# Stick-breaking attention: splitting a pair of heads in one step, with the pieces placed by DMA

## The chip, the cores and the metric

The kernel runs on one core of a Trainium2 chip. The engines of the core are TensorE (PE in the profile; its weight loads are PEld), VectorE (DVE), ScalarE (ACT), GpSimd (POOL) and SyncE (SP), which issues the DMAs. The metric is the device time of one execution in microseconds; the time of a kernel is the median over its runs.

## What is computed

One layer of a hybrid decoder over 1024 tokens of 1024 channels in float32: parallel token mixing (attention, a state-space mixer and two gates), cross-attention into 256 memory tokens, and a dense feed-forward. The change lies in the attention of the first part, 16 heads of 64 channels:

```python
def stick_breaking_attention(q, k, v):
    # beta[t,s] = sigmoid(q_t.k_s / sqrt(d)); A[t,s] = beta[t,s] * prod_{s<j<t}(1 - beta[t,j]), s < t
    ...
    for blk in range(seq // SB_BLOCK):
        z = jnp.einsum('bhtd,bhsd->bhts', qf[:, :, t0:t1], kf[:, :, :t1])
        causal = jnp.arange(t1)[None, :] < (t0 + jnp.arange(SB_BLOCK))[:, None]
        log_1mb = jnp.where(causal, jax.nn.log_sigmoid(-z), 0.0)
        tail = lax.cumsum(log_1mb, axis=3, reverse=True)
        w = jnp.where(causal, jnp.exp(z + tail), 0.0)
        outs.append(jnp.einsum('bhts,bhsd->bhtd', w, vf[:, :, :t1]))
...
merged = jax.nn.sigmoid(ga) * (o_att @ w_br_att[l]) + jax.nn.sigmoid(gs) * (o_ssm @ w_br_ssm[l])
```

q, k and the gate inputs ga and gs are columns of one projection of the normed stream, `h @ w_in`.

## The kernel before

Float32 products are made of several products in the type fp32r. A tensor is split into a high part (a copy rounded to fp32r, mostly by ACT) and a low part (the tensor minus its high part, a subtraction mostly by DVE); `mm3` (L101) multiplies high by high, high by low and low by high.

The attention stage is L725 to L926. It works on eight pairs of heads, and on 1024 positions in two halves of 512.

*Projections.* `dense` (L747) makes 128 output channels, that is one pair of heads, for all positions: it loads and splits the weights, and then runs for each half 8 x 3 matmuls into one PSUM bank ("mm", two banks), after which an eviction function is called with the bank. `qk_proj` (L771) gives it two such functions. `ev_q` (L775) writes for each of the two heads one tile "qs" of 128 partitions: partitions 0 to 63 hold the high part of q (L783, ACT), partitions 64 to 127 its low part (L784, DVE). `ev_k` (L786) writes two tiles for each head: "kh" holds the high part of k in both halves of the partitions, "kl" the low part; ACT (L795) and DVE (L796) write partitions 0 to 63, and a DMA for each tile copies these to partitions 64 to 127 (L797, L798). So one matmul over 128 partitions with qs and kh, and one with qs and kl, give all four products of a score. Each of these eviction instructions handles 64 partitions of 512 elements; each half of q or k has two on ACT and two on DVE. The tiles of q and k have four buffers, two pairs.

*Gates.* `gate_proj` (L802) uses `dense` too; its eviction is a sigmoid on ACT into a tile "gt" (two buffers), which is stored (L806). The last four of the 16 blocks of gate channels (gates 12 to 15) are computed inside the attention stage, beside its last five steps.

*Scores and values.* `scores` (L826) computes for one block of 128 positions the products with the keys (L838, L839), takes the sigmoid on ACT (L840) and a running product by a scan on DVE (L841). `values` (L848) transposes the result with PE (L857), splits it into weights wth (ACT, L860) and wtl (DVE, L861) and multiplies with the differences of v (L869, L870) into the one PSUM bank "av". At the end of a half of a head the two halves of the bank's partitions are added: ACT copies the lower one into a tile with the tag "gt" (L877), DVE adds it into the pair's output tile "oT" (L878, two buffers; one tile for each half of the positions, shared by the two heads), and after the second head SP stores the tile (L880). `differences` (L811) loads v twice, shifted by one position (L817), subtracts on POOL (L818) and splits on POOL (L92, L99).

*Order.* The main loop runs over 32 steps m, a head and a half each; four steps make a pair. `interleave` (L892) mixes the values of step m, the scores of step m + 1 and a quarter of the projections of a later pair (`qk_quanta`, L900): the pair after the next one's first q half in the last step of a pair, then second q half, first k half and second k half in the next three. Pair 0 is projected ahead of the loop, and its projections and those of pair 1 begin before attention proper. From step 27 on the quarters are replaced by pieces of the gates 12 to 15. The instructions of each engine run in the order that a scheduler lays down ahead of the run, from a simulated timeline and the program order; `issue_behind` (L212) keeps the projections from running ahead of the attention matmuls. A tile that takes over a buffer waits until all readers of the tile before it are done, stores among them.

After the attention stage follows the state-space stage (from L935 on), whose first matmul against the decay rows is L1027; its tables are built by POOL (L971) and DVE (L965 to L974) in memory that the attention stage leaves.

Of the kernel before, what the change touches and what calls it, by code (L numbers as in the profile page):

```python
# [8 lines left out]
F32 = mybir.dt.float32  # L9
F32R = mybir.dt.float32r  # L10
# [6 lines left out]
P = 128  # L17
# [4 lines left out]
HALF = 512  # L22
# [13 lines left out]
def hybrid_block(ctx, tc, a, out, dbg=None):  # L36
# [214 lines left out]
    with ExitStack() as pa:  # L251
# [473 lines left out]
        with ExitStack() as p2:  # L725
# [45 lines left out]
            def qk_proj(hp):  # L771
                for j in range(2):
                    heads[2 * hp + j] = {}

                def ev_q(ps, half):  # L775
                    sl = slice(half * HALF, (half + 1) * HALF)
                    for j in range(2):
                        hd = heads[2 * hp + j]
                        if half == 0:
                            hd["q"] = mk(qk, [P, S], F32R, "qs")  # L780
                        pj = ps[j * HD:(j + 1) * HD]
                        q = hd["q"]
                        A.activation(q[0:HD, sl], pj, AF.Copy)  # L783
                        V.tensor_tensor(q[HD:P, sl], pj, q[0:HD, sl].bitcast(F32), ALU.subtract)  # L784

                def ev_k(ps, half):  # L786
                    sl = slice(half * HALF, (half + 1) * HALF)
                    for j in range(2):
                        hd = heads[2 * hp + j]
                        if half == 0:  # L790
                            hd["kh"] = mk(qk, [P, S], F32R, "kh")
                            hd["kl"] = mk(qk, [P, S], F32R, "kl")
                        pj = ps[j * HD:(j + 1) * HD]
                        kh, kl = hd["kh"], hd["kl"]
                        A.activation(kh[0:HD, sl], pj, AF.Copy)  # L795
                        V.tensor_tensor(kl[0:HD, sl], pj, kh[0:HD, sl].bitcast(F32), ALU.subtract)  # L796
                        nc.sync.dma_start(kh[HD:P, sl].bitcast(F32), kh[0:HD, sl].bitcast(F32))  # L797
                        nc.sync.dma_start(kl[HD:P, sl].bitcast(F32), kl[0:HD, sl].bitcast(F32))  # L798

                return dense(C_Q + hp * P, ev_q), dense(C_K + hp * P, ev_k)  # L800

            def gate_proj(gi):  # L802
                def ev(ps, half):
                    gt = mk(t2, [P, HALF], F32, "gt")
                    A.activation(gt, ps, AF.Sigmoid)
                    nc.sync.dma_start(g_d[gi * P:(gi + 1) * P, half * HALF:(half + 1) * HALF], gt)  # L806
                return dense(C_GA + gi * P, ev)
# [40 lines left out]
            def values(h, half, ns_):  # L848

                st = {}  # L850
                ni = 4 * (half + 1)

                def tr(i):
                    t0 = max(0, i - 4 * half)
                    pt = mk(pst, [P, HALF], F32, "tr")
                    for tb in range(t0, 4):
                        T.transpose(pt[:, tb * P:(tb + 1) * P], ns_[tb][:, i * P:(i + 1) * P], ident)  # L857
                    wh = mk(wt, [P, HALF], F32R, "wth")
                    wl = mk(wt, [P, HALF], F32R, "wtl")
                    A.activation(wh[:, t0 * P:], pt[:, t0 * P:], AF.Identity, bias=mone)  # L860
                    V.scalar_tensor_tensor(wl[:, t0 * P:], pt[:, t0 * P:], -1.0, wh[:, t0 * P:].bitcast(F32), ALU.add, ALU.subtract)  # L861
                    st[i] = (wh, wl, t0 * P)

                def av(i):
                    if i == 0:
                        st["po"] = mk(psv, [P, HALF], F32, "av")
                    po, vt = st["po"], heads[h]["v"]
                    wh, wl, off = st[i]
                    T.matmul(po[:, off:], vt[:, i, :], wh[:, off:], start=i == 0, stop=False)  # L869
                    marks.append(T.matmul(po[:, off:], vt[:, i, :], wl[:, off:], start=False, stop=i == ni - 1))  # L870
                    if i == ni - 1:
                        hp, j = h // 2, h % 2
                        if (hp, half) not in ots:
                            ots[hp, half] = mk(t2, [P, HALF], F32, "oT")
                        o = ots[hp, half]
                        tmp = mk(t2, [P, HALF], F32, "gt")[0:HD]
                        A.activation(tmp, po[HD:P], AF.Copy)  # L877
                        V.tensor_tensor(o[j * HD:(j + 1) * HD], po[0:HD], tmp, ALU.add)  # L878
                        if j == 1:
                            nc.sync.dma_start(o_d[hp * P:(hp + 1) * P, half * HALF:(half + 1) * HALF], o)  # L880

                def step(i):
                    def run():
                        if i < ni:
                            tr(i)
                        if i >= LAG:
                            av(i - LAG)
                    return run

                return [step(i) for i in range(ni + LAG)]  # L890
# [976 lines left out]
```

## Time and profile before

| what | value |
|---|---|
| median of 3 runs | 2595.1 us |
| lowest to highest | 2594.28 to 2597.31 us |
| the profiled execution's own time | 2590.97 us |
| its span in the profile | 2589.3 us |
| mean granted PE clock over the span | 0.992 |
| attention main loop | about 675 to 1103 us of the span |

In the profile a row of a timeline gives the start and the duration in us, the engine, the line of the kernel, the operation with the tiles that it writes and reads, and in brackets the idle time of the engine just before it with what ended that. A row of the chain of waits gives the engine and line that waited, what it waited for, the sum of the waits in us, their number and the longest. A row of the summed windows gives the stretch, its length, and then for PE, PEld, DVE, ACT and POOL the busy us with the number of instructions, then the granted PE clock, the mean busy share of the 16 DMA engines and the GB/s that they moved. A row of the groups gives line, engine, operation, tiles, shapes and count, then the busy sum in us, the mean in ns, and the idle time before with its causes.

### The profile page before, as it was taken

How to read it: one execution, taken by the hardware profiler on the slowest of the kernel's cores; microseconds unless marked ns; L12 is line 12 of the kernel's file. 1: busy time of each engine (PE TensorE's matmuls, PEld its weight loads, DVE VectorE, ACT ScalarE, POOL GpSimd, SP SyncE). 2: the span in 40 equal slices, each digit the busy share in tenths (PEclk: the TensorE clock that was granted, in tenths of full speed). 3: DMA queues.
4: the chain of work that ended last, by engine and by line, in shares of the span. 5: the costliest groups of instructions: out<-in, count | busy, mean ns of one | idle time of the engine just before them, and what ended most of it. 6: DMA issues, size and time to landing. Idle time of an engine off the chain costs nothing. (4 is left out here: it accounts for less than half of the span.)

```text
span 2589.3 us, 32651 instructions
## 1 busy us (share of the span) xinstructions
PE 2491.0 (96%) x12026; PEld 2061.8 (80%) x12026; DVE 1824.0 (70%) x2119; ACT 1149.1 (44%) x2052; POOL 881.1 (34%) x690
## 2 busy tenths in 40 slices
PE   8999999999999999979999999999999999999998
PEld 6778787887787788767888788887787888887776
DVE  7676777777588988678788654415459666666997
ACT  6333354655466665556544302314333333334433
POOL 5331544443121211145656231101114323323675
PEclk9999999999999999989999999999999999999999
DMA  6441443334422322255322452321232232234322
GB/s 228 148 141 49 134 145 99 108 98 122 114 74 61 86 66 74 83 167 194 110 90 75 146 175 94 118 62 49 83 117 74 78 98 74 81 98 164 130 98 98
DMA packets 244331, 278.54 MB, mean 108 GB/s; under 512 B 15039, under 2 KB 171848, under 8 KB 243786
## 3 DMA queue, kind: packets, MB, share of 16 engines
q1 hardware_dynamic: 244170, 276.45, 33.6%
q8 instruction: 95, 1.56, 0.2%
q14 instruction: 66, 0.54, 0.1%
HBM read 197.87 MB, written 70.13 MB: 104 GB/s over the span
## 5 line engine op out<-in xcount | busy, mean ns | idle before, releaser
L841 DVE TENSOR_TENSOR_SCAN n<-n,mask 128x128 f32<-128x128 f32 (+7 forms) x128 | 178.5, 1418 | 10.5 <-ACT n L840 9.7
L99 DVE TENSOR_TENSOR sw<-sf,sw 128x512 fp32r<-128x512 f32 x150 | 128.9, 872 | 65.1 <-ACT sw L96 64.5
L196 POOL TENSOR_TENSOR sf<-wr,wr 128x512 f32<-128x512 f32 x38 | 59.5, 1566 | 286.0 <-DMA wr<-in_w_gu_dram 138.4
L860 ACT ACTIVATE wth<-tr,mone 128x512 fp32r<-128x512 f32 x192 | 111.1, 581 | 74.8 <-PE tr L857 73.3
L96 ACT ACTIVATE sw<-sf 128x512 fp32r<-128x512 f32 x150 | 91.9, 626 | 98.6 <-PE mm L222 86.1
L861 DVE SCALAR_TENSOR_TENSOR wtl<-tr,wth 128x512 fp32r<-128x512 f32 x192 | 101.5, 546 | 40.1 <-ACT wth L860 38.7
L99 DVE TENSOR_TENSOR sw<-wr,sw 128x512 fp32r<-128x512 f32 x113 | 107.0, 950 | 31.6 <-ACT sw L96 31.5
L222 PE MATMUL mm<-h,sw 128*128 128x512 f32 x320 | 124.3, 389 | 1.8 <-DVE sw L99 1.8
L220 PE MATMUL mm<-h,sw 128*128 128x512 f32 x320 | 122.3, 390 | 3.1 <-ACT h L96 2.3
L96 ACT ACTIVATE sw<-wr 128x512 fp32r<-128x512 f32 x113 | 70.9, 629 | 122.5 <-PE mm L222 122.2
L221 PE MATMUL mm<-h,sw 128*128 128x512 f32 x320 | 124.5, 389 | 0.0
L102 PE MATMUL mm<-oth,bw 128*128 128x512 f32 (+1 forms) x320 | 122.3, 382 | 2.1 <-DVE a L1138 1.5
L104 PE MATMUL mm<-oth,bw 128*128 128x512 f32 (+1 forms) x320 | 119.2, 372 | 0.6 <-DVE bw L1125 0.4
L103 PE MATMUL mm<-otl,bw 128*128 128x512 f32 (+1 forms) x320 | 118.6, 371 | 0.0
L92 POOL TENSOR_SCALAR v<-va 128x512 fp32r<-128x512 f32 x16 | 21.0, 1317 | 274.9 <-PE av L870 147.9
L656 DVE SCALAR_TENSOR_TENSOR b<-b,prmT,b 128x1023 f32<-128x1023 f32 (+2 forms) x72 | 106.0, 1475 | 10.3 <-ACT b L654 9.8
L840 ACT ACTIVATE n<-sc 128x512 f32<-128x512 f32 (+1 forms) x192 | 89.2, 486 | 49.0 <-PE sc L839 25.2
L165 POOL TENSOR_SCALAR rstd<-ms 128x1 f32<-128x1 f32 x82 | 27.7, 338 | 239.3 <-ACT x L1359 101.5
L102 PE MATMUL p<-bw,h 128*128 128x512 f32 x256 | 98.9, 391 | 3.3 <-DVE x L1361 2.3
L104 PE MATMUL p<-bw,h 128*128 128x512 f32 x256 | 100.1, 392 | 0.0
L103 PE MATMUL p<-bw,h 128*128 128x512 f32 x256 | 99.8, 390 | 0.0
L198 POOL TENSOR_TENSOR sf<-wr 128x512 f32<-128x512 f32 x38 | 63.2, 1663 | 107.4 <-DVE sw L99 107.4
(592 smaller groups left out, 8180.1 us busy)
## 6 DMA issues: line engine op xcount, KB each, us to landing
wr<-in_w_gu_dram SPq DMA_DIRECT2D x80, 256.0 KB
wr<-in_w_in_dram SPq DMA_DIRECT2D x36, 512.0 KB
zr<-in_w_in_dram SPq DMA_DIRECT2D x32, 512.0 KB
gu_d<-t SPq DMA_DIRECT2D x44, 256.0 KB
wraw<-in_w_in_dram SPq DMA_DIRECT2D x20, 512.0 KB
xs_d<-b SPq DMA_DIRECT2D x32, 256.0 KB
s<-xs_d SPq DMA_DIRECT2D x32, 256.0 KB
s<-zs_d SPq DMA_DIRECT2D x32, 256.0 KB
```

The source lines that it names most:

```text
L96: A.activation(o, i, AF.Copy)
L99: eng.tensor_tensor(o, i, hi.bitcast(F32), ALU.subtract)
L102: first = T.matmul(ps, sh, mh, start=start, stop=False)
L103: T.matmul(ps, sh, ml, start=False, stop=False)
L104: T.matmul(ps, sl, mh, start=False, stop=stop)
L220: T.matmul(ps, w[0][:, k, :], b[0][:, k, :], start=first and k == 0, stop=False, skip_group_check=True)
L221: T.matmul(ps, w[0][:, k, :], b[1][:, k, :], start=False, stop=False, skip_group_check=True)
L222: T.matmul(ps, w[1][:, k, :], b[0][:, k, :], start=False, stop=last and k == 3, skip_group_check=True)
L656: V.scalar_tensor_tensor(acc[:, sh:], y[:, :S - sh], cw(3 - sh, f), acc[:, sh:], ALU.mult, ALU.add)
L841: V.tensor_tensor_scan(nt[:, 0:L][:, ::-1], nt[:, 0:L][:, ::-1], mask[:, S - L:][:, ::-1], 1.0, ALU.mult, ALU.max)
L860: A.activation(wh[:, t0 * P:], pt[:, t0 * P:], AF.Identity, bias=mone)
L861: V.scalar_tensor_tensor(wl[:, t0 * P:], pt[:, t0 * P:], -1.0, wh[:, t0 * P:].bitcast(F32), ALU.add, ALU.subtract)
```

## The change

For the pairs 1 to 7 (`hp > 0`) a new function `split` takes the whole bank of 128 partitions, both heads: one ACT copy into a tile "hT" (the high part) and one DVE subtraction into "lT" (the low part), one buffer each. DMAs then carry the pieces of 64 partitions to their places: for q two for each head (high part, low part), for k four for each head (each part into both halves of the partitions). Pair 0 keeps the old way. Tiles with the tags "oT" and "gt", with two buffers each, are replaced by "oT0" and "oT1", one buffer each, for the two halves; the late gates use these same tags, and the ACT copy of the finished output (L877) uses "hT". The sum of these tiles' memory is the same as before.

```diff
@@ qk_proj
+                def split(ps):
+                    hi, lo = [mk(t2, [P, HALF], F32R, n, bufs=1) for n in ("hT", "lT")]
+                    A.activation(hi, ps, AF.Copy)
+                    V.tensor_tensor(lo, ps, hi.bitcast(F32), ALU.subtract)
+                    return hi.bitcast(F32), lo.bitcast(F32)
+
                 def ev_q(ps, half):
                     sl = slice(half * HALF, (half + 1) * HALF)
+                    if hp > 0:
+                        parts = split(ps)
                     for j in range(2):
                         hd = heads[2 * hp + j]
                         if half == 0:
                             hd["q"] = mk(qk, [P, S], F32R, "qs")
-                        pj = ps[j * HD:(j + 1) * HD]
                         q = hd["q"]
-                        A.activation(q[0:HD, sl], pj, AF.Copy)
-                        V.tensor_tensor(q[HD:P, sl], pj, q[0:HD, sl].bitcast(F32), ALU.subtract)
+                        rows_ = slice(j * HD, (j + 1) * HD)
+                        if hp > 0:
+                            for r, t in enumerate(parts):
+                                nc.sync.dma_start(q[r * HD:(r + 1) * HD, sl].bitcast(F32), t[rows_])
+                        else:
+                            A.activation(q[0:HD, sl], ps[rows_], AF.Copy)
+                            V.tensor_tensor(q[HD:P, sl], ps[rows_], q[0:HD, sl].bitcast(F32), ALU.subtract)
 
                 def ev_k(ps, half):
                     sl = slice(half * HALF, (half + 1) * HALF)
+                    if hp > 0:
+                        parts = split(ps)
                     for j in range(2):
...
-                        pj = ps[j * HD:(j + 1) * HD]
                         kh, kl = hd["kh"], hd["kl"]
-                        A.activation(kh[0:HD, sl], pj, AF.Copy)
-                        V.tensor_tensor(kl[0:HD, sl], pj, kh[0:HD, sl].bitcast(F32), ALU.subtract)
-                        nc.sync.dma_start(kh[HD:P, sl].bitcast(F32), kh[0:HD, sl].bitcast(F32))
-                        nc.sync.dma_start(kl[HD:P, sl].bitcast(F32), kl[0:HD, sl].bitcast(F32))
+                        rows_ = slice(j * HD, (j + 1) * HD)
+                        if hp > 0:
+                            for d, t in zip((kh, kl), parts):
+                                for r in range(2):
+                                    nc.sync.dma_start(d[r * HD:(r + 1) * HD, sl].bitcast(F32), t[rows_])
+                        else:
+                            A.activation(kh[0:HD, sl], ps[rows_], AF.Copy)
+                            V.tensor_tensor(kl[0:HD, sl], ps[rows_], kh[0:HD, sl].bitcast(F32), ALU.subtract)
+                            for t in (kh, kl):
+                                nc.sync.dma_start(t[HD:P, sl].bitcast(F32), t[0:HD, sl].bitcast(F32))
@@ gate_proj
-                    gt = mk(t2, [P, HALF], F32, "gt")
+                    gt = mk(t2, [P, HALF], F32, f"oT{half}", bufs=1)
@@ values, av
                         if (hp, half) not in ots:
-                            ots[hp, half] = mk(t2, [P, HALF], F32, "oT")
+                            ots[hp, half] = mk(t2, [P, HALF], F32, f"oT{half}", bufs=1)
                         o = ots[hp, half]
-                        tmp = mk(t2, [P, HALF], F32, "gt")[0:HD]
+                        tmp = mk(t2, [P, HALF], F32, "hT", bufs=1)[0:HD]
```

## The prediction

> **What bounds the kernel now.** I read the page first, then the summed windows over the attention stage, then the chain of waits there, then the timelines of the places the waits point to.
>
> ```profile
> span 2589.3 us, 32651 instructions
> PE 2491.0 (96%) x12026; PEld 2061.8 (80%) x12026; DVE 1824.0 (70%) x2119; ACT 1149.1 (44%) x2052; POOL 881.1 (34%) x690
> ```
> ```profile
> 680.00:1030.00 350.00, 337.47 (x1837) 281.50 (x1836) 308.36 (x374) 216.46 (x421) 60.59 (x39) 1.00 0.26 71
> ```
>
> The change touches the projections of pairs 1 to 7, and these lie between about 680 and 1030 us. There PE is busy 337.47 of 350 us at full granted clock, and DVE 308.36 (88%). Over the whole span DVE is at 70%, so here it is much closer to its limit than on average. What can be won is PE's idle time in the window, 350 - 337.47 = 12.5 us, 0.48% of the span. No saving on DVE or ACT is worth more than that, however many instructions go. The waits of PE in this window:
>
> ```profile
> PE av L870 <- DVE wtl L861: 8.5, 12, 1.2
> PE mm L102 <- DVE qs L784: 2.7, 2, 1.4
> PE tr L857 <- DVE wtl L861: 1.1, 1, 1.1
> ```
>
> They make 12.3 of the 12.5 us, and all end on DVE. So DVE's queue sets the end here, at a few fixed places, while PE's own work sets the rest. The places, one period of a pair (some 50 us) taken as the example; first DVE and PE where the first k half is evicted:
>
> ```profile
> 908.24 0.68 DVE L796 TENSOR_TENSOR kl<-mm,kh 64x512 fp32r<-64x512 f32 x1
> ...
> 911.45 0.69 DVE L796 TENSOR_TENSOR kl<-mm,kh 64x512 fp32r<-64x512 f32 x1
> 912.07 3.66 DVE L841 TENSOR_TENSOR_SCAN n<-n,mask 128x768 f32<-128x768 f32 x2
> 915.76 0.62 DVE L861 SCALAR_TENSOR_TENSOR wtl<-tr,wth 128x256 fp32r<-128x256 f32 x2
> ```
> ```profile
> 890.24 0.39 PE L870 MATMUL av<-wtl,v 128*128 128x256 f32 x1 [0.23 <-DVE wtl L861]
> ...
> 903.25 0.50 PE L102 MATMUL mm<-t1h,whi 128*128 128x512 f32 x1 [1.36 <-DVE qs L784]
> 903.59 0.40 PE L103 MATMUL mm<-t1l,whi 128*128 128x512 f32 x1
> 903.82 0.39 PE L104 MATMUL mm<-t1h,wlo 128*128 128x512 f32 x1
> ...
> 916.24 0.39 PE L870 MATMUL av<-wtl,v 128*128 128x256 f32 x1 [1.23 <-DVE wtl L861]
> ```
>
> At 916.24 PE stood 1.23 us for a weight tile that DVE began at 915.76, behind two scans, behind the second head's k subtraction at 911.45. At 890.24 it is the same with 0.23 us, after the first q half. Twelve such waits sum to 8.5 us with 1.2 as the longest; six of each of the two sizes would be 8.8, so they alternate, one of each in a pair. At 903.25 PE stood 1.36 us for the second head's q subtraction itself, which sat behind a slow scan:
>
> ```profile
> 899.17 3.30 DVE L841 TENSOR_TENSOR_SCAN n<-n,mask 128x512 f32<-128x512 f32 x1
> 902.50 0.70 DVE L784 TENSOR_TENSOR qs<-mm,qs 64x512 fp32r<-64x512 f32 x1
> ...
> 950.55 1.21 DVE L841 TENSOR_TENSOR_SCAN n<-n,mask 128x512 f32<-128x512 f32 x1
> ```
> ```profile
> 898.99 2.40 POOL L818 TENSOR_TENSOR va<-va,vb 128x1024 f32<-128x1024 f32 x1 [4.57 <-DMA va<-v_d]
> ...
> 950.66 3.30 POOL L818 TENSOR_TENSOR va<-va,vb 128x1024 f32<-128x1024 f32 x1 [4.87 <-issue]
> ```
>
> The same scan takes 1.21 us one pair later. It is slow where POOL's subtraction of v began 0.18 us ahead of it, and quick where POOL began 0.11 us behind it; there POOL took 3.30 instead of 2.40.
>
> **The change, part by part.** Evictions. Of each q or k half two copies on ACT and two subtractions on DVE (64 rows each) become one of each with 128 rows.
>
> ```profile
> L784 DVE TENSOR_TENSOR qs<-mm,qs 64x512 fp32r<-64x512 f32 x28 | 19.3, 689 | 2.0 <-ACT qs L783 0.4
> L795 ACT ACTIVATE kh<-mm 64x512 fp32r<-64x512 f32 x28 | 16.6, 594 | 14.3 <-PE mm L104 13.2 <-DVE kl L796 0.7
> L861 DVE SCALAR_TENSOR_TENSOR wtl<-tr,wth 128x512 fp32r<-128x512 f32 x80 | 54.2, 679 | 25.6 <-ACT wth L860 25.1
> ```
> ```profile
> L805 ACT ACTIVATE gt<-mm x8: 588/598/602, 1030.1 to 1099.4; 128x512 f32<-128x512 f32 x8
> ```
>
> On DVE 128 rows of 512 from PSUM cost 0.679 us, 64 rows 0.689; on ACT 0.598 against 0.594. Rows are free, so half of the instructions go: 7 pairs x 4 halves = 28 on DVE x 0.689 = 19.3 us, and 28 on ACT x 0.594 = 16.6 us. On the path is only what stands in front of a PE wait. First k half: the 0.69 us at 911.45 goes from the front of the 1.23 us wait; I take 0.65 x 6 = 3.9 us (bounds 0, if something else fills the place, and 6 x 1.2 = 7.2). First q half: the 0.23 us vanishes, 6 x 0.22 = 1.3 us. Second q half: the two waits of together 2.7 us end on an instruction that is gone, but the transposed-tile work behind it is then next on DVE; I take 2.0 (bounds 0 and 2.7). The one wait of 1.1 us: half, 0.6. Second k half: no wait of PE ends there, so nothing. Sum: 3.9 + 1.3 + 2.0 + 0.6 = 7.8 us, with 0 and 12.5 as ends.
>
> Pieces by DMA. q gets 4 DMAs per half (none before), k 8 (4 before): 24 issues of SP for a pair in place of 8. What they cost is in the existing ones:
>
> ```profile
> 908.23 0.47 SPq L797 DMA_DIRECT2D kh<-kh  x1
> ```
> ```profile
> 908.00:910.00 2.00, 2.00 (x14) 1.70 (x13) 1.86 (x3) 2.00 (x6) 0.00 (x0) 1.00 0.28 65
> 910.00:912.00 2.00, 2.00 (x13) 1.68 (x12) 1.97 (x4) 1.95 (x5) 0.00 (x0) 1.00 0.29 67
> 912.00:914.00 2.00, 2.00 (x11) 1.67 (x10) 2.00 (x3) 1.69 (x4) 0.00 (x0) 1.00 0.59 135
> ```
>
> SP: 16 more x 0.47 = 7.5 us in 50; behind them on SP queue the loads of weights and v and the stores of output tiles, which come later by at most the 3.8 us of one half's eight issues. The DMA engines: 2.0 x (0.28 + 0.29 + 0.59) = 2.32 us for four pieces, 0.58 each; 16 more make 9.3 us in a period in which they are 26% busy. q and k of a pair are read only while the next pairs are worked on, so their landing is covered; without that cover the first scores of a pair would wait 3 to 5 us (next paragraph). Cost taken: 0.
>
> The shared buffer. The high part (hT) has one buffer, and the copy of the finished output (L877) now uses it too. So this copy waits until the pieces of the high part have landed; behind it on ACT stand the high parts of the transposed weights, and PE waits for those. The closest places are the second q half and the second k half:
>
> ```profile
> 895.10 0.57 ACT L783 ACTIVATE qs<-mm 64x512 fp32r<-64x512 f32 x1
> ...
> 901.49 0.59 ACT L877 ACTIVATE gt<-av 64x512 f32<-64x512 f32 x1 [0.69 <-PE av L870]
> ```
> ```profile
> 921.67 0.68 DVE L796 TENSOR_TENSOR kl<-mm,kh 64x512 fp32r<-64x512 f32 x1 [0.18 <-ACT kh L795]
> ```
> ```profile
> 927.77 0.59 ACT L877 ACTIVATE gt<-av 64x512 f32<-64x512 f32 x1 [1.28 <-PE av L870]
> ```
>
> The copy starts 901.49 - 895.67 = 5.8 us after the q high part is ready, and 927.77 - 921.67 = 6.1 us after that of k. Three q issues are 1.4 us, six k issues 2.8 us, and the last piece then needs about 2 us (the traffic of the issues up to 912.21 is over by 914). That is 3.4 and 4.8 us: covered, by 2.4 and 1.3 us. Cost 0; the cover can go (a rival below).
>
> Output tiles with one buffer each. Up to pair 6 nobody else wants oT0 or oT1. At the end the late gates do: gate 14 is evicted into them while pair 7 still holds them.
>
> ```profile
> 1077.10 0.60 ACT L805 ACTIVATE gt<-mm 128x512 f32<-128x512 f32 x1
> ```
> ```profile
> 1089.85 0.38 SPq L880 DMA_DIRECT2D o_d<-oT  x1
> ```
> ```profile
> 1092.76 0.53 POOL L971 MEMSET cb<- 128x512 f32 x1 [6.41 <-PE mm L103]
> ```
> ```profile
> 1099.53 0.75 DVE L974 CAST keyrows<-cb 128x512 fp32r<-128x512 f32 x2
> ```
> ```profile
> 1109.10 1.19 PE L1027 MATMUL dec<-colrows,keyrows 128*128 128x512 f32 x2 [4.28 <-DMA colrows<-sum_d]
> ```
>
> The eviction at 1077.10 must now wait for the store issued at 1089.85 to land, about 1092. Both PSUM banks of the projections are then held by gate 14, so the 48 matmuls of gate 15 (48 x 0.23 = 11 us, by the steps from 903.59 to 903.82) can't run under pair 7's last work. With them out of the way that store comes earlier, I take about 1089, and the last of the 48 ends near 1100 in place of about 1092.7 (when POOL's L971 was let go). L971 moves with it by 7.5 us. Its result is wanted at 1099.53, 6.8 us after its start; with L971 itself and a select between, some 5.5 us of that are slack, so 7.5 - 5.5 = 2 us reach the next stage, whose L1027 starts at 1109.10. Bounds: 0 (PE is idle there for 4.28 us anyway) and 11.
>
> Sum: -7.8 + 2.0 = -5.8 us. The profiled execution took 2590.97 us, its span 2589.3; the median of the three runs is 2595.1, 4.1 above. I carry that difference along: 2595.1 - 5.8 = 2589.3 us.
>
> **The rivals.** *The gates give it back.* The end of the stage costs 6 to 11 us: the chain behind L971 then moves as a whole. For it: all 48 matmuls are displaced for certain. Against: the 5.5 us of slack. Price: -7.8 + 8 = 0, 2595.
>
> *The slow scan in every pair.* POOL's start is within 0.2 us of the scan's in both pairs shown, so any shift can turn it. In six pairs in place of two, four more scans are 3.30 - 1.21 = 2.09 us longer, of which PE showed 1.36 where it was hit: +5.4, and the 2.0 of the second q half is lost: -5.8 + 7.4 = +1.6, 2597. The Trainium skill ("SBUF — State Buffer", section "SBUF: two separate sides") calls the pair of ports that DVE and GpSimd share an exclusive lock: whichever instruction starts first holds it to its end. By that rule the loser is late in every pair and only who loses can change; the trace agrees with both orders (a scan of 3.30 us, a subtraction of 3.30 us).
>
> *Slower: hT holds the output copy.* The second q half's pieces are issued just when v, an output tile and weights are in flight:
>
> ```profile
> 898.00:900.00 2.00, 2.00 (x14) 1.57 (x13) 2.00 (x4) 0.54 (x1) 1.01 (x1) 1.00 0.98 282
> ```
>
> If they queue behind that traffic, which ends at about 900.2, four pieces end at 902.5, 1 us after the copy's turn at 901.49; it decides from a landing later than 5.8 us after the high part. With 1 us at both close places of 7 pairs: 14 us, -5.8 + 14 = +8, 2603.
>
> *The freed time does not reach PE*: something else on DVE fills each place and only the tail's cost is left. 0 to +2, 2596; the two scans at 912.07 speak for some of it.
>
> **How the numbers follow.** About 0.2% (5.2 us) is what a measurement of this kernel can tell from no change. Forecast 0.48: own range -12 to -3; 0.41 of it faster, 0.07 within. Gates 0.17 (0.13 within, 0.04 slower). Slow scan 0.12 (0.10 within, 0.02 slower). hT 0.15 (0.04 within, 0.11 slower). No relief 0.08 (within). Faster 0.41, same 0.42, slower 0.17. The range goes from -13 (all of PE's idle time) to +7.
>
> **What would show it.** Right: 28 fewer evictions on DVE and on ACT between 680 and 1030; PE's idle time there down from 12.5 to about 5 us, its wait for qs gone, that for wtl after the first k half near 0.6; the output copy (L877 before) not waiting for a DMA; the first matmul of the next stage (L1027, now 1109.10) about 6 us earlier, in spite of gates that end later. Wrong: waits of ACT for DMAs that read hT or lT, with PE waiting for ACT behind them; a gap of PE between the last output and the next stage that grows by more than 5 us; scans of 3.3 us in each pair.

## The result and the profile after

The changed kernel takes 2599.26 us (median of 22 runs) where the kernel before takes 2592.93 (22 runs on the same chip): ratio 1.0027, interval [1.0021, 1.0033], so it is slower by some 6.3 us. The forecast was 5.8 us faster. The time lies inside the stated range, on the other side of zero.

The page of the changed kernel, its summed window over the same stretch as before, and PE's chain of waits there. Lines have moved by 19: L860 is the scan (L841 before), L876 the transposes, L879 and L880 the transposed weights, L888 and L889 the value products, L896 the output copy, L897 the output's add, L824 the late gates, L777 and L778 the new split.

```profile
span 2597.2 us, 32736 instructions
```
```profile
680.00:1030.00 350.00, 334.00 (x1803) 278.82 (x1803) 291.19 (x339) 194.50 (x389) 60.17 (x39) 1.00 0.44 109
```
```profile
PE av L889 <- DVE wtl L880: 7.0, 10, 0.9
PE av L888 <- DVE oT L897: 4.2, 7, 0.6
PE tr L876 <- DVE wtl L880: 3.9, 6, 0.8
```

DVE's busy time fell from 308.36 to 291.19 us and ACT's from 216.46 to 194.50: the evictions did go. Yet PE's idle time rose, from 12.5 to 350 - 334.00 = 16.0 us. The waits for qs are gone, as forecast, and the longest for wtl fell from 1.2 to 0.9, where the forecast had 0.6. In their place PE waits for the output's add (L897) and, six times, ahead of the transposes. What is new on ACT and DVE, from their chains of waits in the same stretch:

```profile
ACT hT L777 <- DVE oT L897: 7.3, 12, 1.0
...
ACT hT L777 <- DMA kh<-hT: 3.3, 5, 1.8
...
DVE lT L778 <- DMA kl<-lT: 5.6, 4, 2.7
```

None of these is the wait that the prediction priced: the output copy (L896) waits for no DMA here. It is the split that waits, first for the reader of the output copy (the add), then for the pieces of the split before it. One place in full, from the timeline; it is the second k half of the pair that had its first k half at 861:

```profile
868.30 0.60 ACT L896 ACTIVATE hT<-av 64x512 f32<-64x512 f32 x1 [0.30 <-PE av L889]
...
870.97 0.39 PE L104 MATMUL mm<-b22h,wlo 128*128 128x512 f32 x1
...
876.75 0.60 ACT L896 ACTIVATE hT<-av 64x512 f32<-64x512 f32 x1 [0.18 <-PE av L889]
...
877.52 0.69 DVE L897 TENSOR_TENSOR oT<-av,hT 64x512 f32<-64x512 f32 x1
...
878.24 0.60 ACT L777 ACTIVATE hT<-mm 128x512 fp32r<-128x512 f32 x1 [0.18 <-DVE oT L897]
...
882.59 1.23 SPq L812 DMA_DIRECT2D kl<-lT  x2
...
884.32 0.60 ACT L777 ACTIVATE hT<-mm 128x512 fp32r<-128x512 f32 x1 [0.33 <-DMA kh<-hT]
...
885.70 0.69 DVE L778 TENSOR_TENSOR lT<-mm,hT 128x512 fp32r<-128x512 f32 x1 [0.98 <-DMA kl<-lT]
```

The projection's last matmul (L104) starts at 870.97, and its bank could be split then. But the split stands behind a second output copy (876.75), and that copy's add (877.52) must read hT first: the split comes at 878.24, some 7 us late. The program explains the place: `interleave` puts the output copy of this step at 6.5/7 = 0.93 of the step and this split at 7.5/8 = 0.94, while the other three splits of a pair stand ahead of the copy of their step. In the changed kernel, where the two share hT, the split keeps that place in all six pairs of the window. Its eight pieces are issued until 883.8, so they still hold hT and lT when the next pair's first q half is due, and that split waits for two DMAs (884.32, 885.70). One late split makes the next one late.

Of the twelve waits of the split for the add, six are of 0.18 us, at this place: the loss there is in the order and not in the wait. The other six, of about 1.03, are at the second q half, where the split stands behind the output copy of the step before it:

```profile
744.96 0.69 DVE L897 TENSOR_TENSOR oT<-av,hT 64x512 f32<-64x512 f32 x1
...
745.74 0.60 ACT L777 ACTIVATE hT<-mm 128x512 fp32r<-128x512 f32 x1 [1.03 <-DVE oT L897]
```

Two more things of the prediction's list are in this trace. The slow scan:

```profile
749.32 2.40 POOL L837 TENSOR_TENSOR va<-va,vb 128x1024 f32<-128x1024 f32 x1 [4.67 <-DMA va<-v_d]
749.85 2.95 DVE L860 TENSOR_TENSOR_SCAN n<-n,mask 128x512 f32<-128x512 f32 x1
```

A scan of that size behind POOL's subtraction is slow in five of six pairs, in place of two. They take 2.84 to 3.07 us, in place of 1.2. And the late gates:

```profile
1104.36 0.84 POOL L990 MEMSET cb<- 128x512 f32 x1 [18.17 <-PE mm L103]
...
1110.47 0.60 ACT L824 ACTIVATE oT<-mm 128x512 f32<-128x512 f32 x1 [4.10 <-DMA o_d<-oT]
1116.34 0.60 ACT L824 ACTIVATE oT<-mm 128x512 f32<-128x512 f32 x1 [5.27 <-DMA g_d<-oT]
```

They wait for stores as forecast, and the memset that POOL does once the last of the projections' matmuls are through (L971 before, at 1092.76) comes at 1104.36.

### The profile page after: what moved, and what is told of

The parts are those of the page before. It is cut to its first block, busy times and chain, and to the rows that moved or that the text cites. A ratio compares the mean times of both kernels' runs of the same rounds, so it can differ in the third digit from the quotient of the medians.

```text
span 2597.2 us, 32736 instructions
## 1 busy us (share of the span) xinstructions
PE 2492.4 (96%) x12026; PEld 2065.4 (80%) x12026; DVE 1815.5 (70%) x2091; ACT 1129.1 (43%) x2024; POOL 888.5 (34%) x690
## 5 line engine op out<-in xcount | busy, mean ns | idle before, releaser
L860 DVE TENSOR_TENSOR_SCAN n<-n,mask 128x128 f32<-128x128 f32 (+7 forms) x128 | 188.7, 1497 | 13.2 <-ACT n L859 13.1
L879 ACT ACTIVATE wth<-tr,mone 128x512 fp32r<-128x512 f32 x192 | 111.5, 584 | 78.0 <-PE tr L876 76.1
L880 DVE SCALAR_TENSOR_TENSOR wtl<-tr,wth 128x512 fp32r<-128x512 f32 x192 | 101.8, 544 | 53.2 <-ACT wth L879 52.5
L104 PE MATMUL mm<-oth,bw 128*128 128x512 f32 (+1 forms) x320 | 119.7, 374 | 2.0 <-DVE bw L99 1.2
L92 POOL TENSOR_SCALAR v<-va 128x512 fp32r<-128x512 f32 x16 | 12.2, 762 | 278.7 <-PE av L889 164.5
L876 PE MATMUL tr<-ident,n 128*128 128x128 f32 x576 | 95.6, 274 | 5.2 <-DVE wtl L880 5.2
L104 PE MATMUL p<-bw,h 128*128 128x512 f32 x256 | 100.1, 392 | 0.0
```

Of the source, the lines that this page charges most:

```text
L104: T.matmul(ps, sl, mh, start=False, stop=stop)
L860: V.tensor_tensor_scan(nt[:, 0:L][:, ::-1], nt[:, 0:L][:, ::-1], mask[:, S - L:][:, ::-1], 1.0, ALU.mult, ALU.max)
```

## The experiments

Every experiment was timed in five rounds beside the kernel before on the same chip, whose median there lay between 2592.26 and 2594.03. The table holds the ratios, and from one profile each the time from the first value product to the last (L888, "attention"), from there to the first product with the key rows (L1046), from there to the end, PE's idle time between 680 and 1030, and the number of slow scans (over 2.8 us in place of 1.2) there.

| kernel | us | ratio to before, interval | attention | to key rows | rest | PE idle | slow scans |
|---|---|---|---|---|---|---|---|
| before | 2592.93 | | 406.1 | 11.2 | 1480.2 | 12.5 | 2 |
| e8 (same instruction order) | 2592.61 | 1.0001 [0.9991, 1.0011] | 409.9 | 13.4 | 1481.7 | 16.3 | 4 |
| after | 2599.26 | 1.0027 [1.0021, 1.0033] | 411.1 | 12.6 | 1480.2 | 16.0 | 5 |
| e13 (after again) | 2599.40 | 1.0025 [1.0015, 1.0035] | 413.0 | 12.3 | 1478.3 | 17.7 | 5 |
| e1 | 2602.38 | 1.0034 [1.0022, 1.0046] | 411.1 | 11.8 | 1482.7 | 16.4 | 5 |
| e2 | 2599.03 | 1.0025 [1.0013, 1.0036] | 407.5 | 13.8 | 1477.3 | 13.6 | 2 |
| e3 (no subtraction) | 2600.08 | 1.0028 [1.0016, 1.0040] | 404.5 | 11.7 | 1478.7 | 14.4 | none |
| e4 (no subtraction) | 2604.68 | 1.0048 [1.0033, 1.0063] | 409.6 | 11.9 | 1477.8 | 16.9 | none |
| e5 | 2583.37 | 0.9966 [0.9954, 0.9979] | 401.6 | 13.0 | 1477.9 | 8.2 | 0 |
| e6 | 2582.82 | 0.9961 [0.9948, 0.9973] | 399.1 | 13.5 | 1472.6 | 7.9 | 0 |
| e14 (e6 again) | 2583.75 | 0.9962 [0.9948, 0.9976] | 399.4 | 13.3 | 1475.3 | 9.4 | 1 |
| e7 | 2598.70 | 1.0024 [1.0015, 1.0033] | 413.2 | 10.7 | 1482.5 | 16.8 | 5 |
| e9 | 2597.41 | 1.0013 [1.0001, 1.0025] | 406.6 | 13.2 | 1481.3 | 14.9 | 3 |
| e10 | 2595.00 | 1.0000 [0.9989, 1.0012] | 404.8 | 13.1 | 1479.4 | 10.4 | 2 |
| e11 | 2593.74 | 0.9995 [0.9986, 1.0004] | 406.2 | 13.2 | 1479.8 | 11.6 | 1 |
| e12 | 2614.72 | 1.0089 [1.0066, 1.0112] | 434.4 | 14.2 | 1477.9 | 28.8 | 0 |
| e15 | 2596.24 | 1.0011 [1.0000, 1.0021] | 408.7 | 13.6 | 1477.4 | 15.5 | 5 |

How much one profile can say is in the first two rows. The instructions of e8 stand in the same order on every engine as those of the kernel before, and their medians agree, but the profiled execution of e8 (2600.47 us, 7.9 above its median) is 9.4 us longer in span and 3.8 us in attention. So a difference of a few us between two single profiles is nothing; below, times are compared by medians, and profiles by the number and kind of their waits. Up to about 1025 us the orders fall into groups: before, e2, e8 and e9 are alike, and so are after, e13 and e15, and e5, e6 and e14.

**The tail, and the slow scan.** These are the two rivals that the trace seemed to speak for. e1 takes the late gates off the output tiles:

```diff
-                    gt = mk(t2, [P, HALF], F32, f"oT{half}", bufs=1)
+                    gt = mk(t2, [P, HALF], F32, ("lT", "hT")[half], bufs=1)
```

> The changed kernel, but the late gates are evicted into lT and hT, which are idle by then, and not into oT0 and oT1. Theory 'tail' (gate 14 waits for pair 7's output stores, so gate 15 and the tables of the next stage come late): the last gate matmul is done near 1093 to 1097 us of the span instead of 1104.4, L1046 starts 3 to 5 us earlier than 1117, the time falls by 3 to 4 us from 2599 to about 2595.5. Rival 'shared hT' (all the loss is made between 680 and 1030): nothing after 1030 us gets shorter by more than 1 us, time 2598 to 2600. Both expect the waits before 1030 us unchanged.

Measured 2602.38, not faster than the changed kernel and over both expectations. This did not free the gates, it moved them to two other tiles with one buffer; e15 below does it better.

e2 makes only the second part of the change on the kernel before: the two output tiles with one buffer, used by the late gates too.

```diff
-                    gt = mk(t2, [P, HALF], F32, "gt")
+                    gt = mk(t2, [P, HALF], F32, f"oT{half}", bufs=1)
...
-                            ots[hp, half] = mk(t2, [P, HALF], F32, "oT")
+                            ots[hp, half] = mk(t2, [P, HALF], F32, f"oT{half}", bufs=1)
```

> The kernel before with one part of the change alone: output tiles oT0 and oT1 with one buffer each, used by the late gates too; the evictions of q and k and the copy into its own tile stay as before. Theory 'tail': slower than before by 3 to 4 us (2596 to 2597), with gate 14's sigmoid waiting for stores of oT and POOL's L971 waiting for PE until after 1100 us; the stretch 680 to 1030 us as before. Rival 'shared hT': no more than 1 us slower than before.

Measured 2599.03, 5.9 us over its reference of 2593.14 [3.4 to 9.3]. Read by itself this says that the output tiles cost as much as the whole change and that the split gains nothing. Later runs showed that this reading was wrong.

e3 and e4 leave POOL's subtraction of v out of the kernel before and of the changed kernel, so that no scan can be slowed by it; the values are then not differences.

```diff
-                    G.tensor_tensor(va, va, vb, ALU.subtract)
```

> The kernel before without POOL's subtraction of the shifted v (L818): v is used unsubtracted, so that piece of the computation is left out. Theory 'slow scan' (a scan of 512 that meets this subtraction takes 2.9 to 3.3 us instead of 1.2 and PE waits): all scans of 512 near 1.2 us, PE's two waits for qs gone, 2 to 4 us faster than before. Rival: the scan's delay is hidden by other work, within 1 us of before.

> The changed kernel without POOL's subtraction of the shifted v (L837), that piece of the computation left out in the same way. Theory 'slow scan': the five slow scans between 680 and 1030 us return to 1.2 us, and the time falls by 5 to 8 us from 2599, so that the distance to the kernel before without the subtraction is 2 to 4 us in place of 6.3. Rival 'shared hT' and 'tail' alone: the time falls by no more than the same edit takes from the kernel before, distance 5 to 7 us.

Both came out slower than with the subtraction, 2600.08 and 2604.68, against what was expected; the first value product starts 9.6 and 7.0 us later in them (701.4 and 700.3 us). In both profiles the granted clock is 0.83 between 680 and 700 us, where it is 1.00 with the subtraction, and PE waits there some 5 us for the DMAs of kl; what brings this about is not settled. What they do tell: no scan is slow in e4, and its PE still idles 16.9 us, with the same waits of the split on ACT (lines after the one left out are one lower):

```profile
ACT hT L777 <- DVE oT L896: 7.2, 12, 1.0
```

And the distance between them is 4.6 us, close to the 6.3 with the subtraction; in attention it is 5.1 us without it and 5.0 with it. So the slow scans do not make most of the difference. What was left was that row.

**Who shares what.** e5 changes one name: the output copy gets a slot of the ring of four low weight tiles.

```diff
-                        tmp = mk(t2, [P, HALF], F32, "hT", bufs=1)[0:HD]
+                        tmp = mk(wt, [P, HALF], F32, "wtl")[0:HD]
```

> The changed kernel, but the output copy takes a slot of the low weight tiles' ring (four buffers) in place of hT; nothing else. Theory 'shared hT' (split and output copy hold each other's buffer, and that took the relief back): the split of the second k half no longer comes after the output copy, the waits of ACT's split for the output's add (7.3 us between 680 and 1030) are gone, the stretch from the first to the last value product falls from 411.1 to about 406, and the time from 2599 to about 2595. Rival 'pieces': it is the pieces of the split itself that hold hT and lT until they land (5.6 + 3.3 us of waits): these stay, the stretch stays near 411, the time near 2599. Rival 'redrawn order': the schedule comes out different with every edit and its luck is worth some 5 us; then the time may be anywhere from 2593 to 2603 whatever those waits do.

Measured 2583.37: 8.9 us under the kernel before and some 15 under the changed kernel, nearly four times the 4 us expected of it. The window, ACT's waits and PE's wait for the add, and the place shown above, one pair's second k half:

```profile
680.00:1030.00 350.00, 341.80 (x1866) 287.91 (x1865) 285.28 (x347) 199.56 (x401) 59.72 (x39) 1.00 0.45 114
```
```profile
ACT hT L777 <- PE mm L104: 17.8, 21, 3.0
```
```profile
PE av L888 <- DVE oT L897: 3.2, 6, 0.5
```
```profile
862.26 0.60 ACT L896 ACTIVATE wtl<-av 64x512 f32<-64x512 f32 x1 [0.31 <-PE av L889]
...
864.93 0.39 PE L104 MATMUL mm<-b22h,wlo 128*128 128x512 f32 x1
...
865.36 0.60 ACT L777 ACTIVATE hT<-mm 128x512 fp32r<-128x512 f32 x1 [1.62 <-PE mm L104]
...
871.51 0.60 ACT L896 ACTIVATE wtl<-av 64x512 f32<-64x512 f32 x1 [0.19 <-PE av L889]
```

The split now comes 0.43 us after the start of the last matmul, before the second output copy and not behind it. It waits for nothing but PE: the waits for the add are gone, and so are those for the pieces, although hT and lT still have one buffer each. PE idles 8.2 us in place of 16.0; 3.2 of these are waits for the output's add, which the kernel before did not have. Rival *pieces* falls with this: they held hT and lT only because the split before was late.

e6 also takes the late gates off, into the ring of the high weight tiles:

```diff
-                        tmp = mk(t2, [P, HALF], F32, "hT", bufs=1)[0:HD]
+                        tmp = mk(wt, [P, HALF], F32, "wtl")[0:HD]
...
-                    gt = mk(t2, [P, HALF], F32, f"oT{half}", bufs=1)
+                    gt = mk(wt, [P, HALF], F32, "wth")
```

> The changed kernel, with the output copy in a slot of the low weight tiles' ring and the late gates in slots of the high weight tiles' ring, so that hT holds nothing but the split and the one-buffer output tiles nothing but outputs. Theory 'shared buffers' (hT and the late gates together): the time falls by the 4 us of hT and by the 2 us at the end of the stage, to about 2593, level with the kernel before or below it; the late gates end some 7 us earlier. Rival 'pieces': 2597 (only the 2 us of the end). Rival 'redrawn order': anywhere from 2593 to 2603.

Measured 2582.82, the fastest median of all, but only 0.6 us under e5. Their intervals overlap almost wholly.

e7 is the split alone, with its parts in the two rings of weight tiles and gates, outputs and copy as in the kernel before:

```diff
-                    hi, lo = [mk(t2, [P, HALF], F32R, n, bufs=1) for n in ("hT", "lT")]
+                    hi, lo = [mk(wt, [P, HALF], F32R, n) for n in ("wth", "wtl")]
...
```

> The split alone: the kernel before with both heads split at once and moved by DMA, the high and low parts in slots of the two rings of weight tiles (four buffers each); output tiles, gates and output copy stay in their two-buffer tiles as before. Theory 'shared buffers': with nothing shared the forecast relief arrives, 5 to 8 us under the kernel before, 2586 to 2589. Rival 'pieces': the split gains nothing on its own, 2593 to 2598, since the pieces hold ring slots for 5 us and the weight tiles of the transposes wait for them. Rival 'redrawn order': from 2590 to 2600.

Measured 2598.70. The rival *pieces* named the mechanism, and both chains of waits show it: now it is the weight tiles that wait until the pieces have left their slots. On ACT and on DVE:

```profile
ACT wth L879 <- DMA qs<-wth: 9.9, 3, 4.7
```
```profile
DVE wtl L880 <- DMA qs<-wtl: 16.8, 5, 4.9
```

The output copy bears a ring slot (its reader follows within a few us), the split's parts do not (a queue of pieces reads them). What reads a slot matters, and not only how many there are.

e8 is the other half of e2: output tiles with one buffer each, gates left alone.

```diff
-                            ots[hp, half] = mk(t2, [P, HALF], F32, "oT")
+                            ots[hp, half] = mk(t2, [P, HALF], F32, f"oT{half}", bufs=1)
```

> The kernel before with the output tiles as two tiles of one buffer each and nothing else; gates keep their own two-buffer tile. Theory 'late gates' (the cost of 5.9 us of the output-tile part alone came from the gates evicted into these tiles): no cost is left, 2592 to 2594. Rival 'one buffer': the tiles themselves cost, because the add of the next pair waits for the store of the last: 2597 to 2599 as with the gates. Rival 'redrawn order': anything from 2590 to 2600.

Measured 2592.61 against 2592.26: nothing. The order of the instructions is that of the kernel before. So what e2 cost came with the gates. The profile of e8 also shows how far one order can vary: twice as many slow scans as before, and PE's wait for the second q half with them.

```profile
PE mm L102 <- DVE qs L784: 5.7, 4, 1.5
```

**Is it the split, and which of its halves.** e5 differs from the kernel before in the split, in where the copy lies, and in the output tiles of e2, which gained nothing there. e9 is the control for the copy: the kernel before with only the output copy in the ring.

```diff
-                        tmp = mk(t2, [P, HALF], F32, "gt")[0:HD]
+                        tmp = mk(wt, [P, HALF], F32, "wtl")[0:HD]
```

> The control: the kernel before, with nothing changed but that the output copy takes a slot of the low weight tiles' ring instead of a 'gt' tile. Theory 'the split pays once hT is its own': this does nothing, 2590 to 2595, first to last value product near 406, and the gain of 9 us of the version with the copy in its own slot is the split's. Rival 'the copy's slot pays': the gain comes from where the copy lies and not from the split; then this kernel is near 2584 too, with a stretch near 401.

Measured 2597.41, slower by 0.13% (0.3 to 6.5 us) and not faster, which was not expected either. So the gain of e5 does not come from where the copy lies; it is the split's. The instructions of e9 stand in the order of the kernel before up to 1039 us and in another after that, beside the late gates: an edit that touches no gate redraws the end of the stage, and a few us can come from that alone.

e10 and e11 are e5 with only the k halves, or only the q halves, split for both heads at once; the condition of the other function is made false in both its places. The first place in e10:

```diff
 def ev_q(ps, half):
...
-                    if hp > 0:
+                    if hp > 7:
```

> The changed kernel with the output copy in its own slot, and only the k halves split for both heads at once; the q halves are evicted head by head as before. Theory 'terms of the forecast' (k 3.9 of the relief, q 1.3 + 2.0): 3.5 to 5 us under the kernel before, about 2588; the waits for qs come back (2 of together about 2.7 us), those for wtl after the first k half stay short. Rival 'all or nothing': the relief comes from the order that the whole gives, each half alone gives nothing, 2591 to 2595.

> The same with only the q halves split at once; k is evicted head by head as before. Theory 'terms of the forecast': 2 to 4 us under the kernel before, about 2589; the waits of 1.2 us for wtl after the first k half are there again, six of them, those of 0.23 us and for qs are gone. Rival 'all or nothing': 2591 to 2595.

Measured 2595.00 and 2593.74, both level with the kernel before, so by time neither reaches what I had expected of it. By the waits that go, they are the terms of the forecast one by one. PE's chain of waits with k alone, then with q alone:

```profile
PE av L889 <- DVE wtl L880: 5.4, 12, 0.7
PE mm L102 <- DVE qs L796: 2.7, 2, 1.4
```
```profile
PE av L889 <- DVE wtl L880: 7.2, 6, 1.2
PE av L888 <- DVE oT L897: 2.7, 5, 0.5
```

k alone cuts the long waits from 1.2 to 0.7 and leaves the 2.7 for qs as they were. q alone takes away the waits for qs and the six short ones for wtl, and leaves six of 1.2; but a new one of 2.7 us comes in, for the output's add (L897). PE's idle time is 10.4 and 11.6 us; the four kernels without a split (before, e2, e8, e9), all of one order in that stretch but for its last few us, have 12.5 to 16.3, in the mean 14.3. Against that mean it is 4.0 and 2.7 us less, where the forecast had 3.9 and 3.3; against the profile of before alone it is 2.1 and 0.9, so these sizes are uncertain by some 2 us. Why so little reaches the end with one half alone stays open. Both kernels also hold what cost time on its own, the copy in the ring (e9, 3.4 us) and the gates in the output tiles (e2, 5.9 us).

e12 lets the output copy share lT in place of hT:

```diff
-                        tmp = mk(t2, [P, HALF], F32, "hT", bufs=1)[0:HD]
+                        tmp = mk(t2, [P, HALF], F32, "lT", bufs=1)[0:HD]
```

> The changed kernel, with the output copy in lT, the buffer of the low part, in place of hT, the buffer of the high part. Theory 'the split waits for the copy's reader': ACT's split is free now, but the low part on DVE comes behind the output's add on the same engine, so part of the loss stays: 2588 to 2595. Rival 'any sharing with a one-buffer tile puts the split behind the output copy': as with hT, 2597 to 2602, the second k half evicted after the output copy again. Rival 'only ACT's wait counts': as with a slot of its own, 2582 to 2586.

Measured 2614.72, worse than all three expectations. Here the rival of the prediction, that the output copy is held by pieces, is seen: the copy is the late one. ACT's and PE's chains of waits, and one such place, in order of time:

```profile
ACT lT L896 <- DMA qs<-lT: 26.7, 7, 5.2
```
```profile
PE av L888 <- DVE oT L897: 23.1, 6, 5.0
```
```profile
855.97 1.32 SPq L793 DMA_DIRECT2D qs<-lT  x2
...
863.46 0.59 ACT L896 ACTIVATE lT<-av 64x512 f32<-64x512 f32 x1 [4.01 <-DMA qs<-lT]
...
864.09 0.68 DVE L897 TENSOR_TENSOR oT<-av,lT 64x512 f32<-64x512 f32 x1 [3.91 <-ACT lT L896]
...
864.82 0.50 PE L888 MATMUL av<-wth,v 128*128 128x512 f32 x1 [3.77 <-DVE oT L897]
```

The pieces of the low part are issued last, the copy stands 4.01 us for them, and the one bank of the value products ("av") cannot be started anew before the add has read it, so PE stands 3.77 us. Not all of the time is such waits: from 800 to 1030 us the granted clock of this profile is 0.95, where the changed kernel has 1.00. In these two kernels, whichever user of the one-buffer tile is placed second pays.

**Side by side.** e13 is the changed kernel unaltered, e14 is e6 unaltered, and e15 takes only the late gates out of the changed kernel's output tiles, with the copy still in hT:

```diff
-                    gt = mk(t2, [P, HALF], F32, f"oT{half}", bufs=1)
+                    gt = mk(wt, [P, HALF], F32, "wth")
```

> The changed kernel once more, unaltered, for a second time on another chip and a second profile. Theory 'hT': 5 to 8 us over the kernel before, and in the second profile as in the first a wait of ACT's split for the output's add of about 7 us between 680 and 1030, PE idle there near 16 us. Rival 'chance of one profile': these waits, or the slow scans in five of six pairs, are not there a second time.

> The version with the output copy and the late gates in ring slots once more, beside the changed kernel on the same chip. Theory 'hT': 14 to 17 us under the changed kernel and 8 to 11 under the kernel before, PE idle near 8 us between 680 and 1030, no slow scan. Rival 'chance': the distance to the changed kernel falls under 8 us.

> The changed kernel with only the late gates moved to slots of the high weight tiles' ring; the output copy still shares hT. Theory 'hT alone': nothing comes back, 2597 to 2602, the waits of the split for the output's add stay at about 7 us. Rival 'late gates': the 2 to 6 us that the output-tile part costs when added to the kernel before come back, 2593 to 2596.

Measured 2599.40, 2583.75 and 2596.24 on one chip. The 15.7 us between e13 and e14 hold. The windows of e13 and e14, and the row of the split in e13 and in e15, which is the same to the tenth as in the changed kernel's first profile:

```profile
680.00:1030.00 350.00, 332.34 (x1792) 276.95 (x1791) 291.46 (x337) 193.10 (x384) 58.51 (x38) 1.00 0.44 110
```
```profile
680.00:1030.00 350.00, 340.59 (x1855) 286.31 (x1854) 288.24 (x350) 197.08 (x395) 58.81 (x39) 1.00 0.46 115
```
```profile
ACT hT L777 <- DVE oT L897: 7.3, 12, 1.0
```
```profile
ACT hT L777 <- DVE oT L897: 7.3, 12, 1.1
```

Without the late gates 3.2 us come back, by the medians; 2596.24 lies between what the two expectations say, and the two intervals overlap at their ends, so the size is uncertain. The memset comes 4.1 us before the last value product; in the changed kernel it comes with it (1104.36 and 1104.4):

```profile
1099.31 0.53 POOL L990 MEMSET cb<- 128x512 f32 x1 [7.96 <-PE mm L103]
```

The rest, 12.5 us from e15 to e14, is the output copy in hT. In the profiles 9.3 us of it lie in attention; where the other 3 lie is not shown.

## Why the prediction was wrong

The step that failed is "The shared buffer", with its "Cost 0": the runs put 12.5 us there (e15 to e14). The evictions' sum stood; the late gates have the forecast sign, but not by the way that was forecast.

*Evictions.* Right in the sum, where hT belongs to the split alone: 28 fewer on each engine at the forecast prices, and the relief is there. Attention takes 406.1, 409.9, 406.6 and 407.5 us in the four kernels without a split, in the mean 407.5, and 401.6, 399.1 and 399.4 with the split and hT for itself, in the mean 400.0. That is -7.5 us against the forecast's -7.8. By time it is -8.9 to -9.4 us. Its parts were in the places named: the wait for qs gone, the one after the first k half from 1.2 to 0.7, for which the forecast said 0.6. Not forecast was the new wait for the output's add, 3.2 us in e5; so PE's idle time came down to 8.2, 7.9 and 9.4 us, and not to the 5 of the forecast. The single terms are not shown by time, since neither half alone (e10, e11) is faster than before.

*Pieces by DMA.* Cost 0 was right where hT and lT belong to the split alone: in e5 no split waits for a piece. It is not so by nature: e7 and e12 show 9.9 + 16.8 and 26.7 us of waits for pieces.

*The shared buffer.* The prediction asked one question of it, whether "this copy waits until the pieces of the high part have landed", took the distances from the trace of before, 5.8 and 6.1 us, and found them covered. In the changed kernel that copy indeed never waits for a DMA. But sharing binds both ways: the split must also wait until the add on DVE has read the output copy. The distances had been read off an order that the change itself undid. The split of the second k half moved from ahead of the second output copy to behind it, and its pieces then met the next split. Between the kernels with hT shared (after, e1, e13, e15: 411.1, 411.1, 413.0, 408.7, in the mean 411.0) and those without (400.0) attention differs by 11.0 us, of which a part belongs to the late gates (e15, which has them elsewhere, is the shortest of the four). PE's idle time parts the two groups without overlap, 15.5 to 17.7 us against 7.9 to 9.4. I had priced the one direction (a rival at +8, slower, 0.15) and not the other; that the time still lies in the range is owed to that rival's price and not to its mechanism. e12 shows that the priced direction exists as well.

*The late gates.* Forecast +2.0; by medians they cost 3.2 us in the changed kernel (e13 to e15), 0.6 where hT is free (e5 to e6), and 5.9 on the kernel before (e2 against nothing for e8). The sign is the forecast one. The size is not settled: the instructions near the end of the stage stand in another order in each of these kernels, and e9 shows that such an order can cost 3.4 us by itself. Nor is the way shown: the memset does come later, with the last value product in place of 4 to 5 us before it, but from that product to the key rows it is 13.0 us in the mean of the eight kernels with the gates in the output tiles and 12.6 in the eight with them in other tiles that the split does not use. The 2 us were to reach the next stage there.

By the medians of one chip the way from the kernel before to the changed one is -9.4 us (to e14: the split with hT for itself), +12.5 (to e15: the copy in hT) and +3.2 (to e13: the gates in the output tiles), together +6.2. These are steps of one walk and add up by themselves; that each step has the named cause rests on the waits above.

*The slow scan.* It came true as an event, five pairs in place of two, and not as the cause: e4 has none, and its distance to e3 is nearly that of after to before. The versions with both halves split and hT free (e5, e6, e14) have one or none; but e7, which shares no hT, has five, so what brings it about stays open. By the order that the Trainium skill ("SBUF — State Buffer", section "SBUF: two separate sides") gives, in which the first holds the ports to its end, the scan at 749.85 would have begun at 749.32 + 2.40 = 751.72 and ended 1.21 later, at 752.93. It ended at 752.80: the trace agrees. Who came first can't always be read from the starts: in the kernel before POOL's subtraction at 748.50 began 0.03 us ahead of the scan at 748.53, and yet the scan took 1.21 us and the subtraction 3.44. So the prediction's reading, slow where POOL began first, holds for the two pairs that it showed and not for every pair.

*The gates give it back* is at most a part of the loss. *The freed time does not reach PE* was right that no relief arrived, by luck and for the wrong reason: not that something else fills the place, but that the split itself came late.

Of what was to show it wrong, the first mark hit: waits of ACT for DMAs that read hT or lT. They stood at the split and not, as I had it in mind, at the copy. The second did not hit, since from the last value product to the key rows it is 12.6 us in place of 11.2. The third, slow scans, hit in five of six pairs without being the cause.

## What to carry to other kernels

When an edit lets two users share a tile with one buffer, ask both questions, what the first does to the second and what the second does to the first, and ask them of the order that the new dependence makes, not of the distances in the old trace. Share with a tile whose readers are an engine's next few instructions, not with one that a queue of DMAs reads; here one name, "wtl" for "hT", was worth some 15 us and turned a loss into a gain. And before reading a few us from two profiles, look what two profiles of one program differ by.

## What the runs showed of the hardware

Two kernels with the same order of instructions on every engine, before and e8, gave 2 and 4 slow scans of about 3.3 us in the same six pairs, 2.7 and 5.7 us of PE's waits for the second q half, and 12.5 and 16.3 us of PE's idle time in the same 350. In these two executions POOL or DVE came first in different pairs. I had taken the two slow scans of the one profile for a property of the kernel.
